# PEER: float32 one-hots and single products, sums copied out of PSUM, routing picks by four heads with one operand in PSUM

## The chip, the cores and the metric

The kernel runs on one core of one Trainium2 chip. The metric is the device time of one execution in microseconds (us), lower is better; several executions are taken, and the median is reported.

## The reference, cut to what matters

The program is a small network over 256 tokens of width 1024: an RG-LRU mixer, a PEER layer, a FoX attention mixer, a second PEER layer, and then a block with three branches and a dense FFN. Only the two PEER layers are touched. Each has 16384 experts (128 x 128), 8 heads, and picks 16 experts per head and token:

```python
q = (xc @ q_w).reshape(TOKEN_CHUNK, PEER_HEADS, 2, PEER_HALF)
s1 = jnp.einsum('thd,hnd->thn', q[:, :, 0], subkey1).astype(jnp.float32)
s2 = jnp.einsum('thd,hnd->thn', q[:, :, 1], subkey2).astype(jnp.float32)
v1, i1 = lax.top_k(s1, PEER_TOPK)
v2, i2 = lax.top_k(s2, PEER_TOPK)
cand = (v1[..., :, None] + v2[..., None, :]).reshape(...)
top_s, top_c = lax.top_k(cand, PEER_TOPK)
e1 = jnp.take_along_axis(i1, top_c // PEER_TOPK, axis=-1)
e2 = jnp.take_along_axis(i2, top_c % PEER_TOPK, axis=-1)
expert = e1 * PEER_KEYS + e2
g = jax.nn.softmax(top_s, axis=-1)
u = jnp.take(expert_u, expert, axis=0)
act = jax.nn.gelu(jnp.einsum('thkd,td->thk', u, xc).astype(jnp.float32), approximate=False)
w = (g * act).astype(xc.dtype)
return jnp.einsum('thk,thkd->td', w, jnp.take(expert_v, expert, axis=0))
```

## The kernel before, in words

**Dense evaluation.** The kernel gathers no expert. For every one of 128 rows e of the expert grid it computes the activations of that row's 128 experts for all 256 tokens, applies gelu and keeps them in the SBUF array W (128 partitions x 128 rows x 256 tokens). The routing turns into a matrix of gates of the same shape, which multiplies W, and W then multiplies expert_v. A product of two float32 matrices is made of three float32r matmuls on split operands (hi·hi, hi·lo, lo·hi: `mm3`, `proj`); one row e takes 8 x 3 = 24 matmuls of 128x256. The weights come as 512 KB units over the SP queue (`raw`), ACT rounds them to `whi`, and POOL (or DVE) subtracts to get `wlo` (`Stream`).

**A PEER layer** (`peer`) has four stretches. (1) 16 query tiles are projected; from tile 4 on, `q_scores` multiplies the one before with its subkeys: two matmuls per call with plain float32 operands, 128 moving columns each. (2) The loop `for e in range(P)` runs over rows 0 to 95 (`NL = NLOW = 96`): 24 matmuls, a gelu into `W[:, e]`, and between them routing and one-hot work. (3) Rows 96 to 127 go through two small buffers `act` in the space of x, are multiplied with gates that already lie in W, and for two groups of four tokens per row `low(g)` fetches the gates of rows 0 to 95 from DRAM (`gdram`, on the ACT queue) and multiplies them in on DVE or POOL. (4) W times expert_v accumulates over 128 units.

**Routing** (`routing`) runs for token halves t = 0, 1 on DVE. `sides` takes the best 16 of 128 scores for two lists of a head (max, max_index, match_replace). `heads(t)` then works on all eight heads: five additions of candidates, four `sums` (the best 16 of 54 candidates), and the picks: comparisons `ge`, multiplications into `w` and reductions over 8 x 16 x 16 = 2048 elements a partition, all operands in SBUF. `softmax` makes the gates, and after `WAIT` = 4 turns TensorE transposes the two expert indices and the gate; ACT and DVE copy them into `tp`, the gate as a rounded part and a remainder.

**One-hots** (`onehots`). `make(i)` builds for two tokens A (128x256: is this the first index) with one DVE instruction and `gg` (128x256 for each token: one-hot of the second index times the gate, as rounded part and remainder side by side) with one instruction per token; the iota they compare with lies in a PSUM bank. `use` multiplies: one float32r matmul of 128x256 per token, four tokens (a group) into a `ps2` tile of two banks. The rounded part and the remainder stand in separate columns, so ACT copies one out and DVE adds the other, once for rows 0 to 95 (`stage`, then to `gdram`) and once for rows 96 to 127 (W). A layer has 256 tokens, so 64 groups. At row e = NL - 2 = 94 whatever is left of `onehots` is issued at once.

**What sets the order.** The program text issues instructions in the order of these generators; a planner then fixes each engine's order ahead of time, within dependencies, and the engines run their lists in order. In the text, `route()` advances the routing while a rough clock in the program puts DVE behind TensorE; `due` spreads the groups over the rows that are left (`left / (NL - ENDS - e)` a row, cut to 1.0 behind the loop); at row `SCRATCH` = 58 the rest of the routing is forced, since its scratch space in W begins at that row. `tp` lies in columns 1024 to 2047 of x, `act` in 1536 to 2047: gelu of row 96 may write `act` only when the last one-hot that reads there is made.

Of the kernel before, what the change touches and what calls it, by code (L numbers as in the profile page):

```python
# [22 lines left out]
SCRATCH = 58  # L23
WAIT = 4
LAGS = 1
OHB = (2, 3)
# [290 lines left out]
class Kern:  # L317
# [582 lines left out]
    def peer(self, l, ps, gs, shift=None, tasks=None):  # L900
# [6 lines left out]
        with tc.tile_pool(name="W", bufs=1, side="right", reuse_waits="tile") as wp:  # L907
# [22 lines left out]
            step1, sa = half(c0 + 17, 0, 8), half(c0 + 17, 1, 8)  # L930
            scr = [[half(c0 + 18 + i, j) for j in range(2)] for i in range(2)]
            ge, w = [part(c0 + u, 2048).rearrange("p (h k j) -> p h k j", h=8, k=16) for u in (20, 28)]
            gf = half(c0 + 36, 0)
            sm = half(c0 + 36, 1, 2)[:, :, 0:8]
# [33 lines left out]
            def heads(t):  # L968

                v1, v2 = top[:, 0:16:2], top[:, 1:16:2]  # L970
# [7 lines left out]
                i1, i2 = idx[:, 0:16:2], idx[:, 1:16:2]  # L978
                nc.vector.tensor_copy(step1[:, :, 0:1], i1[:, :, 0:1])
                nc.vector.tensor_sub(step1[:, :, 1:16], i1[:, :, 1:16], i1[:, :, 0:15])  # L980
                yield
                for h in range(0, 8, 2):
                    yield from sums(h)
                nc.vector.tensor_copy(cf, cu)
                sh = [P, 8, 16, 16]

                def pick(out, table):
                    nc.vector.tensor_mul(w, ge, table)
# [4 lines left out]
                def slots(s):  # L993
                    return er[t][:, s].rearrange("p (h k) -> p h k", h=8)
# [4 lines left out]
                yield from pick(sa, self.first_step[:, None, None, :].to_broadcast(sh))  # L999
                yield from pick(slots(0), step1[:, :, None, :].to_broadcast(sh))  # L1000
                nc.vector.tensor_sub(bf, cf, sa)
                nc.vector.tensor_tensor(ge, bf[:, :, :, None].to_broadcast(sh),
                                        self.iota_f[:, None, None, 0:16].to_broadcast(sh), op=ALU.is_equal)
# [3 lines left out]
            def softmax(t):  # L1007
                g3 = gf.rearrange("p (h k) -> p h k", h=8)
                nc.vector.tensor_sub(g3, ts, ts[:, :, 0:1].to_broadcast([P, 8, 16]))
                nc.scalar.activation(g3, g3, AF.Exp)  # L1010
                nc.vector.tensor_reduce(sm[:, 0], g3, axis=AX.X, op=ALU.add)
                nc.vector.reciprocal(sm[:, 1], sm[:, 0])
                nc.vector.tensor_mul(g3, g3, sm[:, 1, :, None].to_broadcast([P, 8, 16]))
                for _ in range(WAIT):
                    yield "wait"
# [3 lines left out]
                o = slice(t * P, (t + 1) * P)  # L1019
# [930 lines left out]
```

## Time and profile before

| | us |
|---|---|
| runs of the kernel before: median (lowest, highest of 3) | 2624.33 (2618.27, 3353.15) |
| the profiled execution's own time | 2615.78 |
| span of its profile | 2613.9 |
| mean granted TensorE clock, of full speed | 0.971 |

The rows below come from this one profiled execution. The matmul durations in rows are latencies of pipelined instructions (about 0.28 us, while one starts every 0.12 us), so rates are read from counts in a window; PE's busy time is the union of them. [...] All instructions share line 225 (a helper that records them), so groups are told apart by tile names: `pb` and `ps` are PSUM tiles, `A` and `g` the one-hots, `x` the staging space, `W` the array W or the scratch in it.

### The profile page before, as it was taken

What the parts mean: (1) busy time and instruction counts of PE and PEld (TensorE: products, weight loads), DVE (VectorE), ACT (ScalarE), POOL (GpSimd) and SP (SyncE); (2) the same over time, 40 slices, a digit from 0 to 9 for tenths busy, and PEclk for the clock granted to TensorE, in tenths of its full rate; (3) what the DMA queues carried; (4) which work ended last, traced back from release to release, by engine and by line L of the source; (5) the groups of instructions that cost most, each with busy time, mean ns of one, the idle gap of its engine ahead of it and who ended that gap; (6) DMA issues with size and microseconds to landing.
All of it is one profiled execution on the core that took longest, in us unless ns stands there. A gap on an engine that the chain in (4) does not pass through costs nothing.

```text
span 2613.9 us, 48560 instructions
## 1 busy us (share of the span) xinstructions
PE 2443.3 (93%) x18984; PEld 2369.2 (91%) x18984; DVE 1887.6 (72%) x3552; ACT 1248.1 (48%) x2028; POOL 994.5 (38%) x600
## 2 busy tenths in 40 slices
PE   6879799997899999999997999899999999999998
PEld 5779799997899999888897999789999998999996
DVE  8797997778778765664779877876555557557774
ACT  3655355553434444554544555435444444444553
POOL 5377777762321200231476877340000015203310
PEclk9889999998999999999998999899999999999999
DMA  7755457677788875542454766686555554365564
GB/s 267 287 164 181 143 168 216 214 210 242 241 307 312 311 241 184 156 151 89 150 166 145 210 212 212 202 282 223 182 182 185 184 174 147 112 195 162 186 184 139
DMA packets 164133, 517.38 MB, mean 198 GB/s; under 512 B 18224, under 2 KB 51136, under 8 KB 162880
## 3 DMA queue, kind: packets, MB, share of 16 engines
q1 hardware_dynamic: 117072, 425.77, 51.5%
q10 hardware_dynamic: 38768, 59.14, 6.6%
q0 software_dynamic: 8064, 29.36, 3.5%
q8 instruction: 149, 2.44, 0.4%
q14 instruction: 80, 0.66, 0.1%
HBM read 484.85 MB, written 29.36 MB: 197 GB/s over the span
## 4 chain that ended last, share of the span: by engine, by line
PE 63%; DVE 17%; DMA 8%; issue 7%; POOL 3%; ACT 1%; ACTq 0%; POOLq 0%; DVEq 0%; SPq 0%
PE pb L225 32%; PE ps L225 31%; DVE W L225 7%; DMA x<-gdram 5%; DVE mraw L225 2%; DVE wlo L225 1%; POOL W L225 1%; DVE hl L225 1%; DVE g L225 1%; DMA raw<-pv 1%; DVE tt L225 1%; DVE x L225 1%; DVE mod_mix L225 1%; POOL wlo L225 1%; DVE A L225 1%
## 5 line engine op out<-in xcount | busy, mean ns | idle before, releaser
L225 ACT CAST whi<-raw 128x1024 fp32r<-128x1024 f32 x741 | 777.2, 1050 | 909.2 <-PE ps L225 309.2
L225 POOL TENSOR_TENSOR wlo<-raw,whi 128x1024 fp32r<-128x1024 f32 x284 | 714.0, 2521 | 433.6 <-ACT whi L225 371.7
L225 DVE TENSOR_TENSOR wlo<-raw,whi 128x1024 fp32r<-128x1024 f32 x473 | 610.3, 1291 | 368.7 <-ACT whi L225 366.0
L225 PE MATMUL pb<-hh,whi 128*128 128x256 f32 (+1 forms) x2832 | 810.2, 288 | 34.2 <-ACT x L225 13.0
L225 PE MATMUL pb<-hl,whi 128*128 128x256 f32 (+1 forms) x2832 | 808.8, 286 | 4.7 <-DVE hl L225 4.6
L225 PE MATMUL pb<-hh,wlo 128*128 128x256 f32 (+1 forms) x2832 | 802.1, 285 | 4.9 <-POOL wlo L225 2.5
L225 PE MATMUL ps<-hh,whi 128*128 128x256 f32 x2416 | 686.8, 285 | 11.7 <-ACT hh L225 6.1
L225 PE MATMUL ps<-hh,wlo 128*128 128x256 f32 x2416 | 686.0, 284 | 11.3 <-DVE wlo L225 7.9
L225 PE MATMUL ps<-hl,whi 128*128 128x256 f32 x2416 | 688.4, 285 | 4.7 <-DVE hl L225 4.7
L225 PEld LDWEIGHTS pb<-hh,whi 128*128 128x128 f32 x2832 | 544.7, 193 | 40.5 <-ACT x L225 17.4
L225 PEld LDWEIGHTS pb<-hl,whi 128*128 128x128 f32 x2832 | 545.5, 193 | 5.8 <-DVE hl L225 5.8
L225 PEld LDWEIGHTS pb<-hh,wlo 128*128 128x128 f32 x2832 | 544.7, 193 | 6.3 <-POOL wlo L225 3.3
L225 PEld LDWEIGHTS ps<-hh,wlo 128*128 128x128 f32 x2416 | 461.1, 191 | 15.6 <-DVE wlo L225 10.6
L225 PEld LDWEIGHTS ps<-hh,whi 128*128 128x128 f32 x2416 | 460.6, 191 | 12.8 <-ACT hh L225 6.6
L225 PEld LDWEIGHTS ps<-hl,whi 128*128 128x128 f32 x2416 | 459.1, 190 | 7.1 <-DVE hl L225 5.7
L225 DVE SCALAR_TENSOR_TENSOR g<-pb,x 128x256 fp32r<-128x256 f32 x512 | 222.6, 476 | 0.0
L225 POOL TENSOR_TENSOR W<-W 128x256 f32<-128x256 f32 x12 | 9.3, 774 | 517.7 <-ACT W L225 517.7
L225 PE MATMUL ps<-g,A 128*128 128x256 f32 x512 | 140.1, 299 | 28.1 <-DVE W L225 24.1
L225 DVE TENSOR_TENSOR A<-pb,x 128x256 fp32r<-128x256 f32 x256 | 107.8, 421 | 54.0 <-PE ps L225 52.9
L225 POOL TENSOR_TENSOR W<-W,x 128x384 f32<-128x384 f32 (+1 forms) x66 | 80.2, 1227 | 125.5 <-DMA x<-gdram 94.9
L225 PEld LDWEIGHTS ps<-g,A 128*128 128x128 f32 x512 | 96.4, 199 | 33.0 <-issue 26.2
L225 DVE TENSOR_TENSOR W<-W,x 128x256 f32<-128x256 f32 (+1 forms) x126 | 88.4, 720 | 35.1 <-DMA x<-gdram 20.5
(398 smaller groups left out, 3009.1 us busy)
## 6 DMA issues: line engine op xcount, KB each, us to landing
raw<-pu SPq DMA_DIRECT2D x256, 512.0 KB, 3.9
raw<-pv SPq DMA_DIRECT2D x256, 512.0 KB, 4.1
gdram<-x ACTq DMA_DIRECT2D x128, 192.0 KB, 3.3
x<-gdram ACTq DMA_DIRECT2D x128, 192.0 KB, 3.8
raw<-w_rest SPq DMA_DIRECT2D x40, 512.0 KB, 3.7
raw<-pq SPq DMA_DIRECT2D x32, 512.0 KB, 4.2
mraw<-mod_mix SPq DMA_DIRECT2D x24, 512.0 KB, 5.5
raw<-fox_qkv SPq DMA_DIRECT2D x24, 512.0 KB, 3.7
```

Of the source, the lines that this page charges most:

```text
L225: return f(*args, **kw)
```

## The change

PEER's one-hots become plain float32: `gg` has only the gate itself (128x128 per token), the product of a token is one float32 matmul of 128 moving columns, a group fills one bank, and ACT copies both parts of it out; DVE's additions go. The gate is no longer split, so one ACT copy fills `tp` (three parts in place of four). `heads(t, q)` works on four heads at a time, as soon as their `sides` are there; each of its two-operand instructions has one operand in PSUM (`v2p`, `i1p`, `sap`, `firstp`, `ge`, `mxp`, and the iota). The scratch shrinks (24.5 rows in place of 36.5) and moves from row 58 to 62, `WAIT` is 12 for t = 0 and stays 4 for t = 1, there are four buffers of A and of g (before: 2 and 3), and `due` is cut to 1.5.

```diff
-SCRATCH = 58
-WAIT = 4
+SCRATCH = 62
+WAIT = (12, 4)
-OHB = (2, 3)
+OHB = (4, 4)
...
-            ge, w = [part(c0 + u, 2048).rearrange("p (h k j) -> p h k j", h=8, k=16) for u in (20, 28)]
+            w = part(c0 + 20, 1024).rearrange("p (h k j) -> p h k j", h=4, k=16)
-            tp = xf[:, 1024:2048].rearrange("p (s t) -> p s t", s=4)
+            tp = xf[:, 1024:1792].rearrange("p (s t) -> p s t", s=3)
...
             def sides(h, t):
-                nc.vector.tensor_copy(idx[:, 2 * h:2 * h + 2], iu[:, 2 * h:2 * h + 2])
...
-            def heads(t):
+            def heads(t, q):
+                hs, hd = slice(4 * q, 4 * q + 4), slice(8 * q, 8 * q + 8)
+                sh = [P, 4, 16, 16]
+                v1, v2 = top[:, hd][:, 0::2], top[:, hd][:, 1::2]
+                nc.vector.tensor_copy(v2p, v2)
...
-                        cand[:, :, o:o + n * nb].rearrange("p h (a b) -> p h a b", b=nb),
-                        v1[:, :, a0:a1, None].to_broadcast([P, 8, n, nb]),
-                        v2[:, :, None, 0:nb].to_broadcast([P, 8, n, nb]), op=ALU.add)
+                        cand[:, hs, o:o + n * nb].rearrange("p h (a b) -> p h a b", b=nb),
+                        v1[:, :, a0:a1, None].to_broadcast([P, 4, n, nb]),
+                        v2p[:, :, None, 0:nb].to_broadcast([P, 4, n, nb]), op=ALU.add)
...
+                nc.vector.tensor_copy(idx[:, hd], iu[:, hd])
+                nc.vector.tensor_copy(i1p, i1)
...
-                nc.vector.tensor_tensor(ge, cf[:, :, :, None].to_broadcast(sh),
-                                        self.first[:, None, None, :].to_broadcast(sh), op=ALU.is_ge)
+                nc.vector.tensor_tensor(ge, cf[:, hs, :, None].to_broadcast(sh),
+                                        firstp[:, None, None, :].to_broadcast(sh), op=ALU.is_ge)
...
             def softmax(t):
-                for _ in range(WAIT):
+                for _ in range(WAIT[t]):
                     yield "wait"
...
-                nc.scalar.copy(tp[:, 0:2, o], ps[:, 0:2 * P].rearrange("p (s t) -> p s t", s=2))
-                hi = oh.tile([P, 2, P], F32R, name="A", bufs=OHB[0])[:, 0]
-                nc.scalar.copy(hi, ps[:, 2 * P:3 * P])
-                nc.scalar.copy(tp[:, 2, o], hi.bitcast(F32))
-                nc.vector.tensor_sub(tp[:, 3, o], ps[:, 2 * P:3 * P], hi.bitcast(F32))
+                nc.scalar.copy(tp[:, :, t * P:(t + 1) * P], ps[:, 0:3 * P].rearrange("p (s t) -> p s t", s=3))
...
             def routing():
-                    yield from heads(t)
+                        if h % 4 == 3:
+                            yield from heads(t, h // 4)
...
                 def make(i):
-                    A = oh.tile(b2, F32R, name="A", bufs=OHB[0])
-                    gg = oh.tile([P, 2, 2, P], F32R, name="g", bufs=OHB[1])
+                    A = oh.tile(b2, F32, name="A", bufs=OHB[0])
+                    gg = oh.tile(b2, F32, name="g", bufs=OHB[1])
...
-                        nc.vector.scalar_tensor_tensor(gg[:, k], both, tp[:, 1, n:n + 1],
-                                                       tp[:, 2:4, n, None].to_broadcast(b2),
+                        nc.vector.scalar_tensor_tensor(gg[:, k], io, tp[:, 1, n:n + 1],
+                                                       tp[:, 2, n, None].to_broadcast([P, P]),
...
                 def use():
-                    if i % 2 == 0:
-                        bank[0] = self.ps2()
+                    g = i // 2
+                    bank = picked[:, g % 2 * 512:g % 2 * 512 + 512]
-                        nc.tensor.matmul(bank[0][:, o * T:(o + 1) * T], A[:, k], gg[:, k].rearrange("p s e -> p (s e)"),
-                                         start=True, stop=True)
+                        nc.tensor.matmul(bank[:, o * P:(o + 1) * P], A[:, k], gg[:, k], start=True, stop=True)
...
-                        for o, e in ((st, slice(0, NL)), (W[:, NL:, 4 * g:4 * g + 4], slice(NL, P))):
-                            nc.scalar.copy(o, pv[:, 0, e])
-                            nc.vector.tensor_add(o, o, pv[:, 1, e])
+                        nc.scalar.copy(st, pv[:, 0:NL])
+                        nc.scalar.copy(W[:, NL:, 4 * g:4 * g + 4], pv[:, NL:])
...
+                consts = self.bank(spare)
+                io, firstp, mxp = consts[:, 0:P], consts[:, 128:144], consts[:, 144:152]
+                v2p, i1p, sap = [consts[:, o:o + 64].rearrange("p (h k) -> p h k", h=4) for o in (192, 256, 320)]
+                picked = self.ps2()
+                ge = self.ps2().rearrange("p (h k j) -> p h k j", h=4, k=16)
...
-                        due = min(due, 1.0)
+                        due = min(due, 1.5)
```

## Rows read from the trace of the kernel before

**Rows 1.** The page, part 1: busy us (share of the span) xinstructions, per engine.

```profile
PE 2443.3 (93%) x18984; PEld 2369.2 (91%) x18984; DVE 1887.6 (72%) x3552; ACT 1248.1 (48%) x2028; POOL 994.5 (38%) x600
```

**Rows 2.** Busy time by stretch, PE PEld DVE ACT POOL, PEclk, DMA; first PEER layer.

```profile
core 0: us, PE busy (x) PEld busy (x) DVE busy (x) ACT busy (x) POOL busy (x), PEclk, DMA share, GB/s
220.00:260.00 40.00, 40.00 (x341) 40.00 (x340) 23.56 (x110) 21.63 (x50) 30.24 (x13) 1.00 0.61 198
...
256.30:583.50 327.20, 310.97 (x2551) 310.03 (x2550) 278.02 (x779) 171.96 (x320) 242.84 (x96) 0.97 0.63 189
583.50:612.00 28.50, 15.25 (x79) 13.01 (x78) 25.05 (x61) 8.93 (x20) 0.74 (x1) 0.65 0.58 172
612.00:704.40 92.40, 85.30 (x687) 82.69 (x687) 72.33 (x82) 36.71 (x56) 39.73 (x33) 1.00 0.84 270
...
390.00:575.00 185.00, 185.00 (x1551) 184.98 (x1550) 142.88 (x372) 105.90 (x210) 137.48 (x58) 1.00 0.71 214
```

**Rows 3.** The same view, second PEER layer.

```profile
1332.20:1659.00 326.80, 310.48 (x2552) 309.53 (x2551) 277.68 (x780) 171.95 (x320) 243.09 (x96) 0.97 0.62 190
1659.00:1687.00 28.00, 15.70 (x81) 13.46 (x80) 25.29 (x62) 8.93 (x20) 0.26 (x1) 0.65 0.63 181
1687.00:1778.40 91.40, 85.33 (x685) 83.67 (x684) 71.55 (x81) 38.92 (x60) 40.26 (x33) 0.98 0.83 267
```

**Rows 4.** PE in order of time, 285:328: start, duration, instruction, idle before and releaser.

```profile
287.06 0.39 PE L225 MATMUL pb<-hh,whi 128*128 128x256 f32 x1 [2.09 <-ACT W L225]
308.57 0.44 PE L225 MATMUL pb<-ident,W 128*128 128x128 f32 x1 [8.31 <-DVE W L225]
...
326.71 0.58 PE L225 MATMUL pb<-hh,whi 128*128 128x256 f32 x1 [4.59 <-DVE x L225]
```

**Rows 5.** PE in order of time, 590:613.

```profile
592.84 1.19 PE L225 MATMUL ps<-g,A 128*128 128x256 f32 x4 [3.81 <-DVE W L225]
598.19 1.19 PE L225 MATMUL ps<-g,A 128*128 128x256 f32 x4 [4.16 <-DVE W L225]
600.85 2.00 PE L225 MATMUL ps<-g,A 128*128 128x256 f32 x4 [1.46 <-ACT x L225]
605.71 1.20 PE L225 MATMUL ps<-g,A 128*128 128x256 f32 x4 [2.86 <-DVE W L225]
```

**Rows 6.** Waits, 625:720: engine and tile, releaser, us in total, times, longest.

```profile
POOL W L225 <- DMA x<-gdram: 41.6, 19, 3.9
PEld pb L225 <- ACT x L225: 9.7, 13, 1.8
```

**Rows 7.** PE in order of time, 222:246: plain float32 matmuls of q_scores.

```profile
222.75 0.60 PE L225 MATMUL pb<-W 128*128 128x128 f32 x4
...
245.90 0.60 PE L225 MATMUL pb<-W 128*128 128x128 f32 x4
```

**Rows 8.** DVE groups by shape, 390:575: busy us, mean ns, idle before and releaser.

```profile
L225 DVE SCALAR_TENSOR_TENSOR g<-pb,x 128x256 fp32r<-128x256 f32 x185 | 80.4, 476 | 0.0
L225 DVE TENSOR_TENSOR A<-pb,x 128x256 fp32r<-128x256 f32 x93 | 39.3, 423 | 24.7 <-PE ps L225 24.3
L225 DVE TENSOR_TENSOR x<-x,ps 128x384 f32<-128x384 f32 x46 | 25.2, 548 | 0.2 <-ACT x L225 0.2
L225 DVE TENSOR_TENSOR W<-W,ps 128x128 f32<-128x128 f32 x47 | 13.4, 286 | 18.5 <-ACT W L225 18.5
```

**Rows 9.** DVE in order of time, 284:352: two-operand instructions, both operands in SBUF.

```profile
285.84 4.04 DVE L225 TENSOR_TENSOR W<-W,first 128x2048 f32<-128x2048 f32 x1
...
294.47 2.21 DVE L225 TENSOR_TENSOR W<-W 128x128 f32<-128x128 f32 x1
...
342.86 0.32 DVE L225 TENSOR_TENSOR W<-W 128x128 f32<-128x128 f32 x1
...
346.37 2.28 DVE L225 TENSOR_TENSOR W<-W,first 128x2048 f32<-128x2048 f32 x1
```

**Rows 10.** DVE's waits, 220:260.

```profile
DVE W L225 <- ACT W L225: 15.1, 10, 3.0
```

More of the change, by code (lines that the diff above doesn't have):

```diff
@@ L929, in peer @@
             cf, bf = half(c0 + 16, 0, 8), half(c0 + 16, 1, 8)
-            step1, sa = half(c0 + 17, 0, 8), half(c0 + 17, 1, 8)
+            step1 = half(c0 + 17, 0, 8)
             scr = [[half(c0 + 18 + i, j) for j in range(2)] for i in range(2)]
-            ge, w = [part(c0 + u, 2048).rearrange("p (h k j) -> p h k j", h=8, k=16) for u in (20, 28)]
-            gf = half(c0 + 36, 0)
-            sm = half(c0 + 36, 1, 2)[:, :, 0:8]
+            w = part(c0 + 20, 1024).rearrange("p (h k j) -> p h k j", h=4, k=16)
+            gf = half(c0 + 24, 0)
+            sm = half(c0 + 24, 1, 8)[:, :, 0]
             act = xf[:, 1536:2048].rearrange("p (s t) -> p s t", s=2)
-            tp = xf[:, 1024:2048].rearrange("p (s t) -> p s t", s=4)
+            tp = xf[:, 1024:1792].rearrange("p (s t) -> p s t", s=3)
             def stage(g, n):
@@ L966, in sums @@
                 yield from tops([ts[:, i] for i in r], [cu[:, i] for i in r], [cand[:, i] for i in r], CAND, scr[0])
-            def heads(t):
-                v1, v2 = top[:, 0:16:2], top[:, 1:16:2]
+            def heads(t, q):
[3 more added lines that the diff above has]
+                nc.vector.tensor_copy(v2p, v2)
                 for a0, a1, nb, o in RANKS:
@@ L973, in heads @@
                     nc.vector.tensor_tensor(
-                        cand[:, :, o:o + n * nb].rearrange("p h (a b) -> p h a b", b=nb),
-                        v1[:, :, a0:a1, None].to_broadcast([P, 8, n, nb]),
-                        v2[:, :, None, 0:nb].to_broadcast([P, 8, n, nb]), op=ALU.add)
+                        cand[:, hs, o:o + n * nb].rearrange("p h (a b) -> p h a b", b=nb),
+                        v1[:, :, a0:a1, None].to_broadcast([P, 4, n, nb]),
+                        v2p[:, :, None, 0:nb].to_broadcast([P, 4, n, nb]), op=ALU.add)
                     yield
-                i1, i2 = idx[:, 0:16:2], idx[:, 1:16:2]
-                nc.vector.tensor_copy(step1[:, :, 0:1], i1[:, :, 0:1])
-                nc.vector.tensor_sub(step1[:, :, 1:16], i1[:, :, 1:16], i1[:, :, 0:15])
+                nc.vector.tensor_copy(idx[:, hd], iu[:, hd])
+                i1, i2 = idx[:, hd][:, 0::2], idx[:, hd][:, 1::2]
+                d1 = step1[:, hs]
+                nc.vector.tensor_copy(i1p, i1)
+                nc.vector.tensor_copy(d1[:, :, 0:1], i1[:, :, 0:1])
+                nc.vector.tensor_sub(d1[:, :, 1:16], i1[:, :, 1:16], i1p[:, :, 0:15])
                 yield
-                for h in range(0, 8, 2):
+                for h in range(4 * q, 4 * q + 4, 2):
                     yield from sums(h)
-                nc.vector.tensor_copy(cf, cu)
-                sh = [P, 8, 16, 16]
+                nc.vector.tensor_copy(cf[:, hs], cu[:, hs])
                 def pick(out, table):
-                    nc.vector.tensor_mul(w, ge, table)
+                    nc.vector.tensor_tensor(w, ge, table, op=ALU.mult)
                     yield
@@ L993, in slots @@
                 def slots(s):
-                    return er[t][:, s].rearrange("p (h k) -> p h k", h=8)
-                nc.vector.tensor_tensor(ge, cf[:, :, :, None].to_broadcast(sh),
-                                        self.first[:, None, None, :].to_broadcast(sh), op=ALU.is_ge)
+                    return er[t][:, s].rearrange("p (h k) -> p h k", h=8)[:, hs]
+                nc.vector.tensor_tensor(ge, cf[:, hs, :, None].to_broadcast(sh),
+                                        firstp[:, None, None, :].to_broadcast(sh), op=ALU.is_ge)
                 yield
[L999 to L1003, printed above, removed]
+                yield from pick(sap, self.first_step[:, None, None, :].to_broadcast(sh))
+                yield from pick(slots(0), d1[:, :, None, :].to_broadcast(sh))
+                nc.vector.tensor_sub(bf[:, hs], cf[:, hs], sap)
+                nc.vector.tensor_tensor(ge, bf[:, hs, :, None].to_broadcast(sh),
+                                        io[:, None, None, 0:16].to_broadcast(sh), op=ALU.is_equal)
                 yield
@@ L1108, in peer @@
                 spare = self.ring.pop(0)
-                io = self.bank(spare)[:, 0:P]
+                consts = self.bank(spare)
+                io, firstp, mxp = consts[:, 0:P], consts[:, 128:144], consts[:, 144:152]
+                v2p, i1p, sap = [consts[:, o:o + 64].rearrange("p (h k) -> p h k", h=4) for o in (192, 256, 320)]
                 nc.vector.tensor_copy(io, self.iota_f)
+                nc.vector.tensor_copy(firstp, self.first)
+                picked = self.ps2()
+                ge = self.ps2().rearrange("p (h k j) -> p h k j", h=4, k=16)
                 nc.sync.dma_start(sk, a[f"sk_{l}"].rearrange("p (h n) -> p h n", h=16))
```

19 lines of the change are left out of this document (9 added, 10 removed).

## The prediction

> **What bounds the kernel now.** Part 1 of the page comes first: TensorE is busy 93% of the span, DVE 72%, ACT and POOL less than half [rows 1]. That average does not say what one PEER layer is bound by, so I cut the layer into stretches [rows 2] and looked at how many matmuls start in each. From 390 to 575 us TensorE is busy all of the time at full clock and starts 1551 matmuls in 185.00 us, one every 0.1193 us; DVE is busy 142.88 us of it. This is the steady state of the row loop with one-hot products in it, and TensorE is its bound. The reader should take that rate as a ruler: a stretch's length less its matmuls times 0.1193 us is TensorE time lost. For the first layer that gives
>
> - rows 0 to 95, 256.3 to 583.5: 327.2 - 2551 x 0.1193 = 22.9 us lost;
> - the tail, 583.5 to 612: 28.5 - 79 x 0.1193 = 19.1 us lost;
> - the rows from 96 on, 612 to 704.4: 92.4 - 687 x 0.1193 = 10.4 us lost.
>
> The second layer repeats it with 22.3, 18.3 and 9.7 us [rows 3]. Next I asked what TensorE waited for. In the first stretch the two largest gaps are 8.31 us before a transpose of the routing results, which DVE had not finished, and 4.59 us before a projection whose PSUM bank was held until DVE had copied the gate's remainder into `tp` (DVE x) [rows 4]; the rest is 2.09 us for a gelu, small gaps, and matmuls at half clock after them (mean clock 0.97 [rows 2]). In the tail there are hardly any projections left to run: TensorE multiplies four products and waits again for DVE, 3.81, 4.16, 2.86 us [rows 5], while DVE is busy 25.05 of 28.50 us and the mean clock falls to 0.65 [rows 2]. These are groups that the text had issued by row 94 and that came after it in TensorE's list. In the last stretch the waits are for gates on their way back from DRAM (41.6 us on POOL) and for ACT's gelu [rows 6].
>
> **Part 1, the product: a cost.** A token's product was one float32r matmul of 256 columns, 0.1193 us in the steady state. It becomes one plain float32 matmul of 128 columns. The kernel before has the same thing in `q_scores`: two such matmuls, profiled as four records, once per query tile. From 222.75 to 245.90 us seven tiles pass, 3.307 us each [rows 7]; 24 projections take 24 x 0.1193 = 2.863, which leaves 0.444 us for two, 0.222 us for one. The additional cost is 0.103 x 256 = 26.3 us a layer, **52.6 us in all**. It lies wholly on the path, as TensorE is the bound there. The ends: 0 if a plain product costs what the old one does, and 0.325 us x 256 = 83 us a layer if the products meet the half clock (0.444 us). I take the row of `q_scores`, which stands in the same kind of stream, at full clock.
>
> **Part 2, DVE's share of a group: hidden.** 185 products are 46.25 groups, so DVE spent 142.88 / 46.25 = 3.09 us on a group, and a group came every 4.00 us. The two additions (0.548 + 0.286) go; an instruction for `g` (0.476) shrinks to 128 elements, between 0.286 (another 128x128 instruction that reads PSUM) and 0.476 [rows 8]. Two of A and four of g then make 2 x 0.423 + 4 x 0.286 = 2.0 us, at the worst 2.75. I take 2.0, as that row has the same size and operand. ACT's two copies stay as they are. Nothing of this is a gain in the steady state, where DVE already waits 24.3 us for TensorE [rows 8]; it decides whether the tail remains.
>
> **Part 3, the tail: a gain.** TensorE gets slower per group (0.48 to 0.89 us) and DVE faster (3.1 to 2.0), so DVE is no longer what the groups run behind. 64 groups over some 70 rows is 0.9 a row, 2.86 + 0.8 = 3.7 us of TensorE against 1.8 of DVE. The larger cut of `due` (1.5) lets a delayed group be caught up. I let 2 us of the tail stay (the last copies before `act` comes free): gain 17.1 + 16.3 = **33.4 us**. The ends are 0 and 37.4.
>
> **Part 4, routing: a gain.** The transposes of t = 0 move 8 turns further back in TensorE's list, 8 x 2.86 = 23 us of projections, where the wait was 8.31 us. Queued behind the transposes on TensorE are the projections, and for their results wait ACT's `tp` copy and the first one-hots: those start later, which the rates of part 3 allow. The bank of the transposes is now freed by ACT alone, so the 4.59 us go. DVE also comes earlier: while the queries are projected it waits 15.1 us for scores [rows 10], and the first four heads' additions and picks can stand there. The picks were five two-operand instructions of 2048 elements per half of the tokens with both operands in SBUF, 2.28 us at best and 4.04 otherwise; a 128x128 one took 0.32 and once 2.21 [rows 9]. The new ones have one operand in PSUM and half the elements; between 0 and 5 x 1.76 = 8.8 us per half may be won. Against that stand some 34 more small instructions a layer, at most 0.32 us each, 11 us. Both lie on DVE beside TensorE's projections and I count them as nothing; if that cover were gone, they would come in at +11 to -18 us a layer. Of the 22.9 and 22.3 us I let 4 stay, for the gelu gap of 2.09 and a first wait for one-hots: gain **37.2 us**, with ends 0 and 45.2.
>
> **Part 5, nothing.** Rows 96 to 127 keep their 10.4 and 9.7 us: the same 64 fetches on the ACT queue, the same POOL and DVE products. The tail let a few of them run ahead; I bound that by 5 us a layer in either direction. The other scratch rows, the buffer counts and the smaller `tp` move no work that is late.
>
> **The sum.** 52.6 - 33.4 - 37.2 = -18.0 us against the profiled execution: 2615.8 - 18.0 = **2598 us**. The profiled execution lies just below the lowest of the three runs shown (2618.27) and 8.5 us below their median, 2624.33; I forecast for an execution like it.
>
> **The rivals.**
> - *The tail stays* (slower). Each engine's order is fixed ahead, and nothing in the rows shows that DVE's load made the tail: DVE waited for TensorE in the steady state [rows 8], so it may be the order alone. Then 2615.8 + 52.6 - 37.2 = 2631 us. For it: TensorE had work all the time before the tail. Against it: DVE was busy 88% of the tail. It decides once more than 18.0 / 33.4 = 54% of the tail remains.
> - *Routing stalls as well*: the transposes meet DVE just as late, eight rows on. With the tail that is 2615.8 + 52.6 = 2668 us. Against it: the wait of 8.31 us is shorter than 23 us.
> - *The product is no dearer than before*: 2598 - 52.6 = 2545 us. Only rows 7 speak, and they speak against it.
> - *All stalls go*, with 5 us a layer in the rows from 96 on: 2598 - 4 - 8 - 10 = 2576 us. For it: DVE loses much of its load.
> - [...]
>
> **How the numbers follow.** The forecast gets 0.68, with a range of its own of 2582 to 2614 (what stays of the stalls, and the product at 0.20 to 0.25 us). The tail that stays gets 0.15, both stalls 0.05, a product at the old price 0.04, all stalls gone 0.06, four passes 0.02. The range for 8 in 10 is 2572 to 2640: it takes in the case with the tail and the one without any stall, and leaves out the rest. A change of 2%, 52 us, is about what a measurement of this kernel can tell from none: below 2563 lies only the cheap product (0.04), above 2668 four passes and half of the case with both stalls (0.05), 0.91 between them. In words: a few us gained where TensorE waited, most of it paid back in dearer products.
>
> **What would show it.** The new product: between two of them in the stream some 0.22 us, and two records each. DVE's busy time in the row loop falls by about a third, the additions are gone from its groups. The clock in the row loop stays at 1.00, with no gap of 8.31 or 4.59 us before a transpose or the projection behind it. After row 95 the projections of rows 96 and on run on, with no stretch in which TensorE waits for DVE between products. From the end of the last query tile to the first product with expert_v it is 448.1 us today; I expect about 438. I am wrong if that stretch still holds a block of products after row 95, or if the products cost under 0.2 or over 0.25 us.

## The result, and the profile after

The changed kernel takes 2586.04 us (median of 4 runs, 2585.15 to 2592.58); the kernel before, run beside it, 2622.52 (4 runs, lowest 2618.27). The ratio is 0.9872, 95% interval [0.9847, 0.9896]; it leaves out one run of the kernel before that took 3353.15 us, 28% longer than the others. Between the two profiled executions it is 2585.15 against 2615.78 us, 30.6 us less, where 18 had been forecast.

The page of the kernel after, part 1, answers to [rows 1]:

```profile
PE 2473.5 (96%) x19496; PEld 2406.7 (93%) x19496; DVE 1688.1 (65%) x3364; ACT 1242.3 (48%) x2018; POOL 966.5 (37%) x596
```

TensorE is busy 30 us longer and the span is 31 us shorter: what it stood idle has gone down by some 60 us. The busy time by stretch of the kernel after, both PEER layers, shows where. The columns are those of [rows 2], PEclk the granted clock as a share of full speed; the first line is rows 0 to 95, the second rows 96 to 127, the third lies inside the first, and the last two are the second layer:

```profile
core 0: us, PE busy (x) PEld busy (x) DVE busy (x) ACT busy (x) POOL busy (x), PEclk, DMA share, GB/s
260.30:592.00 331.70, 331.70 (x2817) 331.54 (x2816) 183.63 (x674) 173.60 (x329) 227.60 (x96) 1.00 0.63 194
592.00:691.00 99.00, 92.71 (x753) 90.30 (x752) 81.77 (x93) 41.02 (x63) 40.97 (x32) 1.00 0.88 283
390.00:575.00 185.00, 185.00 (x1577) 185.00 (x1576) 82.58 (x271) 98.15 (x193) 121.45 (x52) 1.00 0.61 192
1316.30:1648.00 331.70, 331.70 (x2817) 331.54 (x2816) 184.38 (x676) 173.81 (x330) 227.78 (x96) 1.00 0.62 192
1648.00:1747.10 99.10, 92.13 (x750) 89.94 (x750) 81.07 (x92) 40.61 (x62) 43.68 (x32) 1.00 0.87 281
```

From the last query tile to the first product with expert_v it is 430.7 us (260.3 to 691.0), where it was 448.1; in the second layer 430.8, where it was 446.2. That is 17.4 + 15.4 = 32.8 us; the rest of the program takes 2.2 us more.

Rows 0 to 95 are now a stretch in which TensorE never stands still. 96 x 24 projections at 0.1193 us are 274.9 us, 256 products at 0.222 us are 56.8, together 331.7, the length of the stretch: nothing is lost, where 22.9 us and, in the tail, 19.1 us were lost. In rows 96 to 127, 99.0 - 32 x 24 x 0.1193 = 7.4 us are lost, where it was 10.4.

TensorE in order of time, kernel after:

```profile
309.01 0.49 PE L225 MATMUL pb<-ident,W 128*128 128x128 f32 x3
313.97 0.61 PE L225 MATMUL ps<-g,A 128*128 128x128 f32 x4
...
581.75 1.05 PE L225 MATMUL ps<-g,A 128*128 128x128 f32 x8
```

The transposes of t = 0 start at 309.01, hardly later than the 308.57 of [rows 4], but with nothing idle before them; the last products start at 581.75, before row 95, so there is no block of products after the row loop as in [rows 5].

DVE's groups by shape, 390 to 575, kernel after, to be read beside [rows 8]:

```profile
L225 DVE SCALAR_TENSOR_TENSOR g<-pb,x 128x128 f32<-128x128 f32 x176 | 52.9, 342 | 0.0
L225 DVE TENSOR_TENSOR A<-pb,x 128x256 f32<-128x256 f32 x88 | 37.0, 421 | 100.4 <-PE ps L225 100.4
```

The additions are gone, and DVE spends 82.58 us of 185 there, where it was 142.88. The last stretch still has the waits of [rows 6] (600 to 691, kernel after):

```profile
POOL W L225 <- DMA x<-gdram: 46.0, 22, 4.1
```

### The profile page after: what moved, and what is told of

The parts are those of the page before. It is cut to its first block, busy times and chain, and to the rows that moved or that the text cites. A ratio compares the mean times of both kernels' runs of the same rounds, so it can differ in the third digit from the quotient of the medians.

```text
span 2583.3 us, 49235 instructions
## 1 busy us (share of the span) xinstructions
PE 2473.5 (96%) x19496; PEld 2406.7 (93%) x19496; DVE 1688.1 (65%) x3364; ACT 1242.3 (48%) x2018; POOL 966.5 (37%) x596
## 4 chain that ended last, share of the span: by engine, by line
PE 71%; DVE 9%; DMA 7%; issue 7%; POOL 3%; ACT 1%; ACTq 0%; POOLq 0%; DVEq 0%
PE pb L225 37%; PE ps L225 34%; DMA x<-gdram 4%; DVE mraw L225 2%; DVE wlo L225 2%; DMA raw<-pv 1%; POOL W L225 1%; DVE W L225 1%; DVE hl L225 1%; DMA mraw<-mod_ffn 1%; POOL wlo L225 1%; ACT whi L225 1%; DVE mod_mix L225 1%; DVE tt L225 1%; DMA raw<-pu 0%
## 5 line engine op out<-in xcount | busy, mean ns | idle before, releaser
L225 POOL TENSOR_TENSOR wlo<-raw,whi 128x1024 fp32r<-128x1024 f32 x282 | 681.5, 2418 | 481.0 <-ACT whi L225 429.6
L225 DVE TENSOR_TENSOR A<-pb,x 128x256 f32<-128x256 f32 x256 | 107.0, 418 | 255.7 <-PE ps L225 223.8
L225 DVE SCALAR_TENSOR_TENSOR g<-pb,x 128x128 f32<-128x128 f32 x512 | 153.6, 341 | 0.0
L225 PE MATMUL ps<-g,A 128*128 128x128 f32 x1024 | 138.3, 274 | 0.0
L225 PEld LDWEIGHTS ps<-g,A 128*128 128x128 f32 x1024 | 127.0, 191 | 0.0
L225 POOL TENSOR_TENSOR W<-W,x 128x384 f32<-128x384 f32 x64 | 85.5, 1345 | 101.3 <-DMA x<-gdram 98.3
L225 ACT COPY x<-ps 128x384 f32<-128x384 f32 x128 | 61.4, 479 | 103.5 <-PE ps L225 103.3
```

Source lines behind the costliest of these rows:

```text
L225: return f(*args, **kw)
```

## The experiments

Three questions were open. Is it the product at 0.222 us that pays most of the gain back? Did the tail go because DVE has less to do? Which part of the routing's change took its stalls away? All times below are medians, with their ratio to the kernel before on the same chip; between runs on different chips the ratios are the fairer comparison. "..." marks where lines of an edit or of a view are left out.

### Each half of the change alone

The kernel before with the new one-hots, products and copies (`make`, `use` and the copy into `tp` are those of the kernel after); its routing stays, by eight heads and in SBUF. The edit to the kernel before, beside these:

```diff
-OHB = (2, 3)
+OHB = (4, 4)
...
-            tp = xf[:, 1024:2048].rearrange("p (s t) -> p s t", s=4)
+            tp = xf[:, 1024:1792].rearrange("p (s t) -> p s t", s=3)
```

> The kernel before with the new one-hots, products and sums alone; routing, its place in the order and the cut of due stay as before. Theory (DVE's share of a group made the tail, the order of the routing made the stalls): the tail of 19 us a layer is gone, the routing stalls of 22 us a layer stay, the dearer products cost 26 us a layer: 2615.8 + 52.6 - 37 = 2631 us, with the gap of 8.3 us before the first transpose still in the trace and no block of products after row 95. Rival (the order alone made the tail, DVE's share did not): nothing is won and the products are paid, 2668 us, with a tail of some 30 matmuls or more after row 95.

2623.8 us, ratio 1.0016 [0.9999, 1.0032]. TensorE in order of time:

```profile
308.77 0.45 PE L225 MATMUL pb<-ident,W 128*128 128x128 f32 x1 [8.30 <-DVE W L225]
...
361.04 1.50 PE L225 MATMUL ps<-g,A 128*128 128x128 f32 x8 [2.18 <-DVE g L225]
...
598.07 1.05 PE L225 MATMUL ps<-g,A 128*128 128x128 f32 x8
```

The routing's stall of 8.3 us stands as before. The last products come at 598.07 with no idle time before them: the tail has gone with this half alone. What it saves pays for the dearer products, and no more.

The routing alone; `ge`, whose tile of two banks the old products use here, lies in SBUF, and each pick's table in PSUM in its place. The edit to the kernel after, beside the old `make`, `use` and copies into `tp`:

```diff
-OHB = (4, 4)
+OHB = (2, 3)
...
+                stepp = consts[:, 152:168]
+                d1p, i2p = [consts[:, o:o + 64].rearrange("p (h k) -> p h k", h=4) for o in (384, 448)]
...
-                yield from pick(slots(0), d1[:, :, None, :].to_broadcast(sh))
+                yield from pick(slots(0), d1p[:, :, None, :].to_broadcast(sh))
```

> The changed kernel with the old one-hots, products (float32r, 256 columns, gate in two parts) and additions on DVE; routing by four heads, waits of 12 and 4, scratch at row 62 and cut of 1.5 as changed. The comparisons ge lie in SBUF here, since the products need the PSUM, and the tables they are multiplied with lie in PSUM instead. Theory: the stalls of the routing go (45 us), the tail stays, since DVE still spends 3.1 us on a group: 2615.8 - 45 = 2571 us. Rival (the order alone made the tail): tail and stalls go and the products cost what they did before, 2586 - 52.6 = 2533 us, which would be faster than both kernels.

2619.2 us, ratio 0.9986 [0.9972, 1.0]: no gain either. TensorE in order of time:

```profile
463.00 0.39 PE L225 MATMUL pb<-hh,whi 128*128 128x256 f32 x1 [1.35 <-ACT W L225]
468.66 0.33 PE L225 MATMUL pb<-ident,W 128*128 128x128 f32 x1 [2.52 <-DVE W L225]
472.30 0.47 PE L225 MATMUL pb<-ident,W 128*128 128x128 f32 x1 [3.31 <-DVE W L225]
474.74 0.58 PE L225 MATMUL pb<-hh,whi 128*128 128x256 f32 x1 [1.96 <-ACT W L225]
...
589.96 1.19 PE L225 MATMUL ps<-g,A 128*128 128x256 f32 x4 [4.72 <-DVE W L225]
...
597.53 1.19 PE L225 MATMUL ps<-g,A 128*128 128x256 f32 x4 [2.87 <-DVE W L225]
```

The stall before the first transposes is gone and the tail stays, as the edit has it. But the gain in the first rows comes back in the transposes of t = 1, which row 62 forces: TensorE waits 1.35 + 2.52 + 3.31 + 1.96 = 9.1 us there for a DVE that has the second half's routing and the old one-hots to do. So the halves change the time by +0.16% and -0.14%, and together by -1.28%. As I read the rows, the light one-hots make the room in DVE that the second routing needs: with them TensorE has no such wait in the kernel after.

### Which part of the routing's change

`WAIT` back to 4 for both halves of the tokens, in the kernel after:

```diff
-WAIT = (12, 4)
+WAIT = (4, 4)
```

> The changed kernel with a wait of 4 turns for both token halves. Theory (the place of the transposes in TensorE's list made the largest stall, together with DVE's lateness): a gap of up to 8 us comes back before the first transposes, with half-clock matmuls behind it, 2586 + 2 x 10 = 2606 us at most. Rival (DVE is early enough by the picks in fours, whatever the wait): no gap, 2586 us within 3.

2589.59 us, ratio 0.988 [0.9855, 0.9906], inside the interval of the change itself. One gap comes back:

```profile
291.14 0.33 PE L225 MATMUL pb<-ident,W 128*128 128x128 f32 x1 [3.05 <-DVE W L225]
```

The transposes are issued 18 us earlier than in the kernel after and wait 3.05 us: DVE is done with the routing at about 291, not at 308. The longer `WAIT` takes that wait away; 3.6 us in the medians is within what the runs can tell from none.

The kernel after with all operands of the picks in SBUF, still by four heads:

```diff
-            w = part(c0 + 20, 1024).rearrange("p (h k j) -> p h k j", h=4, k=16)
+            ge, w = [part(c0 + u, 1024).rearrange("p (h k j) -> p h k j", h=4, k=16) for u in (20, 24)]
...
-                io, firstp, mxp = consts[:, 0:P], consts[:, 128:144], consts[:, 144:152]
-                v2p, i1p, sap = [consts[:, o:o + 64].rearrange("p (h k) -> p h k", h=4) for o in (192, 256, 320)]
+                io = consts[:, 0:P]
+                firstp, mxp = self.first, half(c0 + 29, 1)[:, 0:8]
+                v2p, i1p, sap = [half(c0 + u, i)[:, 0:64].rearrange("p (h k) -> p h k", h=4) for u, i in ((17, 1), (28, 1), (29, 0))]
...
-                ge = self.ps2().rearrange("p (h k j) -> p h k j", h=4, k=16)
```

> The changed kernel with every operand of the picks in SBUF (the picks still by four heads, ge and its neighbours in scratch); only the one-hots still read their iota from PSUM. Theory (the operand in PSUM saves time on DVE alone, beside TensorE's projections): DVE's two-operand instructions of 1024 elements go from about 1.2 us to between 1.2 and 3 us, POOL's subtractions stretch in the same place, and the time stays at 2586 us within 5. Rival (contention of DVE and POOL makes the weights late): TensorE waits for wlo or for the transposes while the picks run, 2595 us or more.

2650.12 us, ratio 1.0109 [1.0083, 1.0134]: 64 us more than the kernel after, and slower than the kernel before. TensorE, ACT, DVE and POOL in order of time, of this kernel:

```profile
290.04 0.58 PE L225 MATMUL pb<-hh,whi 128*128 128x256 f32 x1 [8.71 <-ACT W L225]
...
323.04 0.69 PE L225 MATMUL pb<-ident,W 128*128 128x128 f32 x2 [5.50 <-DVE W L225]
...
343.80 0.80 PE L225 MATMUL ps<-g,A 128*128 128x128 f32 x2 [13.63 <-DVE g L225]
```

```profile
287.04 0.31 ACT L225 ACTIVATE W<-W 128x128 f32<-128x128 f32 x1 [11.69 <-DVE W L225]
```

```profile
288.73 3.07 DVE L225 TENSOR_TENSOR W<-W,first 128x1024 f32<-128x1024 f32 x1
...
327.20 1.21 DVE L225 TENSOR_TENSOR W<-W,first 128x1024 f32<-128x1024 f32 x1
```

```profile
290.99 28.30 POOL L225 TENSOR_TENSOR wlo<-raw,whi 128x1024 fp32r<-128x1024 f32 x10 [0.28 <-ACT whi L225]
...
344.51 2.37 POOL L225 TENSOR_TENSOR wlo<-raw,whi 128x1024 fp32r<-128x1024 f32 x1 [22.83 <-ACT whi L225]
```

And the same picks in the kernel after, with `ge` in PSUM:

```profile
284.00 1.20 DVE L225 TENSOR_TENSOR W<-ps,first_step 128x1024 f32<-128x1024 f32 x1
...
291.73 1.20 DVE L225 TENSOR_TENSOR W<-ps,W 128x1024 f32<-128x1024 f32 x1
```

One instruction, two durations: it took 3.07 us while POOL made `wlo`, 1.21 us at 327, when POOL stood still (its next instruction, at 344.51, has waited 22.83 us). With an operand in PSUM it took 1.20 us with POOL at work. This is where two SBUF operands cost the time: on DVE, and from there on TensorE, which waits 8.71 + 5.50 + 13.63 = 27.8 us in this layer. The first of these comes by way of ACT: the exponential of `softmax` had stood 11.69 us in ACT's list for DVE's input, and the gelu and the rounding of weights stood behind it.

Eight heads at a time as in the kernel before, but one operand of each pick in PSUM, on top of the first experiment:

```diff
-                yield from pick(slots(1), i2[:, :, None, :].to_broadcast(sh))
+                yield from pick(slots(1), i2p[:, :, None, :].to_broadcast(sh))
...
+                more = self.ps2()
+                v2p, i1p, step1, i2p, sap = [more[:, o:o + P].rearrange("p (h k) -> p h k", h=8) for o in range(0, 640, P)]
```

> The kernel of the first experiment (new products, routing by eight heads, waits of 4, scratch at row 58), where now each two-operand instruction of the picks has one operand in PSUM (tables in PSUM, ge in SBUF). Theory (the operand in PSUM makes the routing early, the cut in fours does little by itself): the gap of 8.3 us before the transposes shrinks below 4 us, the time falls from 2624 to 2600 us or less. Rival (it is the cut in fours, which uses DVE's idle time while the queries are projected): 2612 us or more.

2597.55 us, ratio 0.9928 [0.9903, 0.9952], 26 us under the first experiment (23 by the ratios):

```profile
307.62 0.45 PE L225 MATMUL pb<-ident,W 128*128 128x128 f32 x1 [3.48 <-DVE W L225]
...
321.82 0.33 PE L225 MATMUL pb<-ident,W 128*128 128x128 f32 x1 [1.12 <-DVE W L225]
```

Of the 38 us between the first experiment and the kernel after, the operand in PSUM is some 25; fours, `ge` in PSUM and the constants share the rest, and they were not taken apart further, but for the constants:

```diff
-WAIT = (12, 4)
+WAIT = (4, 4)
...
-OHB = (4, 4)
+OHB = (2, 3)
...
-                        due = min(due, 1.5)
+                        due = min(due, 1.0)
```

> The changed kernel with the order constants of before: waits of 4 and 4, buffers of A and g 2 and 3, due cut to 1.0. Theory (operands and sizes made the gain, the constants do not): 2590 us within 5, as with the wait of 4 alone. Rival (fewer buffers and the smaller cut let the groups fall behind): a block of products after row 95, 2600 us or more.

2588.91 us, ratio 0.9895 [0.9864, 0.9926]. Buffer counts, the cut of `due` and `WAIT` together make no difference that these runs can measure.

### The price of the product

The kernel after with A and g as float32r. The gates' lower bits are left out (they are rounded, with no remainder); each product stays 128 columns wide:

```diff
-                    A = oh.tile(b2, F32, name="A", bufs=OHB[0])
-                    gg = oh.tile(b2, F32, name="g", bufs=OHB[1])
+                    A = oh.tile(b2, F32R, name="A", bufs=OHB[0])
+                    gg = oh.tile(b2, F32R, name="g", bufs=OHB[1])
```

> The changed kernel with A and g as float32r: one float32r matmul of 128 columns a token. It leaves out the lower bits of the gate, which is rounded. Theory (the float32 product stands on the path at its full price, since TensorE is busy without a gap in the row loop): a token's product falls from 0.22 to some 0.11 us, 512 of them, and the time with it: 2586 - 56 = 2530 us. Rival (with cheaper products DVE's one-hots or POOL's subtractions become the bound): less than half of that, 2560 us or more.

2527.17 us, ratio 0.9649 [0.9628, 0.967], 59 us under the kernel after. Busy time by stretch, and the group of the products in it:

```profile
390.00:575.00 185.00, 185.00 (x1565) 184.92 (x1564) 91.55 (x268) 104.40 (x204) 132.41 (x58) 1.00 0.70 222
```

```profile
L225 PE MATMUL ps<-g,A 128*128 128x128 f32 x172 | 24.9, 260 | 0.0
```

The ruler gives both prices. Here 172 products stand among 1565 matmuls; the other 1393 are projections but for 3 transposes, so a product takes (185 - 1390 x 0.1193) / 172 = 0.11 us. In the kernel after, 1577 records hold 352 of products, two each: (185 - 1225 x 0.1193) / 176 = 0.221 us. So a plain float32 product costs twice what a float32r one of the same width costs, and the 512 products cost 512 x 0.11 = 56 us more than rounded ones, close to the 59 measured. It all lies on the path. This is the fastest kernel here, but with gates of fewer bits; no kernel with whole gates was measurably faster than the changed one.

### Why the tail went

DVE's additions back into the kernel after. ACT's copies stay, and DVE adds zeros from PSUM to what they leave, two instructions a group as before:

```diff
-                        nc.scalar.copy(st, pv[:, 0:NL])
-                        nc.scalar.copy(W[:, NL:, 4 * g:4 * g + 4], pv[:, NL:])
+                        for o, e in ((st, slice(0, NL)), (W[:, NL:, 4 * g:4 * g + 4], slice(NL, P))):
+                            nc.scalar.copy(o, pv[:, e])
+                            nc.vector.tensor_add(o, o, zp[:, 0:e.stop - e.start].rearrange("p (e o) -> p e o", o=1).to_broadcast([P, e.stop - e.start, 4]))
...
+                zp = consts[:, 384:480]
+                nc.vector.memset(zp, 0.0)
```

> The changed kernel with two more DVE instructions for each group: after each of the two copies out of PSUM, a zero from PSUM is added, in the size and place of the old additions. Theory (DVE's share of a group made the tail): DVE goes from about 1.8 to 2.6 us of the 3.6 to 4 us that a group has, so it still keeps up, no block of products stands after row 95 and the time stays at 2586 us within 8. Rival (the additions themselves, between copy and store, hold a group up, whatever DVE's load): the tail is back, 2610 us or more.

2676.03 us, ratio 1.0214 [1.0191, 1.0238], 90 us more than the kernel after; the theory had it unchanged. Busy time by stretch, DVE's group of the first addition (390 to 575), and TensorE after the row loop:

```profile
390.00:575.00 185.00, 179.73 (x1477) 178.48 (x1476) 98.36 (x323) 90.23 (x173) 119.21 (x50) 0.97 0.60 180
600.00:640.00 40.00, 30.72 (x144) 25.14 (x143) 34.70 (x101) 9.53 (x26) 1.36 (x2) 0.66 0.55 167
```

```profile
L225 DVE TENSOR_TENSOR x<-x,pb 128x384 f32<-128x384 f32 x34 | 18.8, 552 | 81.4 <-ACT x L225 81.2
```

```profile
618.95 2.43 PE L225 MATMUL ps<-g,A 128*128 128x128 f32 x8 [0.74 <-ACT W L225]
...
634.78 2.43 PE L225 MATMUL ps<-g,A 128*128 128x128 f32 x8 [0.74 <-ACT W L225]
```

There is a tail again, and a longer one (12 of the 64 groups come after row 95, seven in the kernel before), though DVE is busy only 98.36 of 185 us. It is not short of time: it stands 81.2 us at the addition, which waits for ACT's copy, which waits for TensorE's products; and behind the addition in DVE's list stand the one-hots of the next products. A quarter of the groups is lost to that round (34 additions of `stage`, so 34 groups, in 185 us; in the kernel after 176 products, 44 groups), and what is left over comes behind the loop.

To tell the wait from the work, the same additions are issued one group later, when the copies have long been made (`flush` holds the two additions and the store to `gdram` of the group that has waited longest). The edit to the kernel with the additions back:

```diff
-                        for o, e in ((st, slice(0, NL)), (W[:, NL:, 4 * g:4 * g + 4], slice(NL, P))):
+                        if ready:
+                            flush()
+                        for o, e in parts:
                             nc.scalar.copy(o, pv[:, e])
-                            nc.vector.tensor_add(o, o, zp[:, 0:e.stop - e.start].rearrange("p (e o) -> p e o", o=1).to_broadcast([P, e.stop - e.start, 4]))
-                        nc.scalar.dma_start(self.gdram[:, g], st.rearrange("p e t -> p (e t)"))
+                        ready.append((g, pv, st, parts))
...
```

> The run with the additions put back (2676 us), with each group's two additions and its store issued one group later, so that DVE meets them when ACT's copies are long done. The same work. Theory now (the wait for the hand-over made the tail): DVE's wait of 81 us in 185 us for ACT's copies is nearly gone and the time falls to 2600 us or less. Rival (the additions cost by their number, or by the planner's order alone): 2650 us or more.

2584.51 us, ratio 0.9868 [0.9838, 0.9898]: as fast as the kernel after, with two more instructions in each of 128 groups.

```profile
390.00:575.00 185.00, 185.00 (x1577) 185.00 (x1576) 125.10 (x401) 97.66 (x193) 122.14 (x52) 1.00 0.63 193
```

```profile
L225 DVE TENSOR_TENSOR x<-x,pb 128x384 f32<-128x384 f32 x44 | 24.3, 553 | 1.8 <-ACT x L225 1.1
```

DVE now works 125.10 us of the same stretch, 27 more than in the run with the tail, and there is no tail. In this form the wait makes it, not the load. The edit moves the store with the additions, and the store waits for them in ACT's list; which of the two lists that stood still costs more was not taken apart.

The load by itself, the other way round: the kernel after with `g` built 256 wide (only the first half is used), no additions, buffers as before:

```diff
-OHB = (4, 4)
+OHB = (2, 3)
...
-                    gg = oh.tile(b2, F32, name="g", bufs=OHB[1])
+                    gg = oh.tile([P, 2, 2, P], F32, name="g", bufs=OHB[1])
...
```

> The changed kernel with each g built 256 wide, as before, the second half unused, and no additions (buffers 2 and 3, which cost nothing in the run with the old constants). DVE's busy time per group rises by about as much as the two additions took, but no DVE instruction waits for ACT. Theory now (not DVE's load but the additions made the tail: DVE's list stands still at them until TensorE and ACT have handed the group over): no block of products after row 95, 2586 us within 8. Rival (the forecast's own step, DVE's load per group): products after row 95 and 2610 us or more, as with the additions put back.

2599.67 us, ratio 0.9932 [0.9905, 0.9959], 13.6 us above the kernel after, more than expected. The stretch has no idle time, and a remnant of a tail stands after row 95, which ends at 589 us (four groups):

```profile
390.00:575.00 185.00, 185.00 (x1574) 185.00 (x1572) 110.96 (x301) 97.05 (x190) 124.19 (x53) 1.00 0.62 191
```

```profile
602.05 1.16 PE L225 MATMUL ps<-g,A 128*128 128x128 f32 x8 [1.12 <-ACT W L225]
```

From the last query tile to the first product with expert_v the layers take 433.6 and 434.8 us, 3 and 4 us more than in the kernel after; the other half of the 13.6 us lies outside them and is not explained. Nor is the remnant put down to load alone: with the additions one group later DVE is busier (125.10 us against 110.96) and no product comes after row 95, but the buffers there are four and four.

Last, the same delay by one group in the old form: the routing alone, above, with its additions (old products, whole gates) one group later. The edit to that kernel:

```diff
-                        for o, e in ((st, slice(0, NL)), (W[:, NL:, 4 * g:4 * g + 4], slice(NL, P))):
+                        if ready:
+                            flush()
+                        for o, e in parts:
                             nc.scalar.copy(o, pv[:, 0, e])
-                            nc.vector.tensor_add(o, o, pv[:, 1, e])
-                        nc.scalar.dma_start(self.gdram[:, g], st.rearrange("p e t -> p (e t)"))
+                        ready.append((g, pv, st, parts))
...
```

> The second experiment (new routing, old products at 0.12 us, gate in two parts, additions on DVE) with the additions issued one group later. It computes all that the kernel before does. Theory now: the tail of the second experiment (products up to 607 us, after row 95) goes, and with it most of 19 us a layer: 2619 - 35 = 2584 us, or down to 2540 us if the 10 us of routing stalls a layer at 463 to 481 us go as well and DVE keeps up. Rival (DVE at 3.1 us a group is too slow beside a group every 3.6 us, whatever the waits): the tail stays, 2610 us or more.

2601.22 us, ratio 0.9939 [0.9918, 0.9959]: 18 us under the routing alone, 12 by the ratios, and between the two theories. From the last query tile to the first product with expert_v it is 439.2 + 437.2 us in the two layers, where it was 445.8 + 442.2.

```profile
390.00:575.00 185.00, 178.06 (x1467) 177.18 (x1466) 146.09 (x381) 97.98 (x191) 131.25 (x56) 0.98 0.65 198
```

```profile
468.47 0.33 PE L225 MATMUL pb<-ident,W 128*128 128x128 f32 x1 [2.97 <-DVE W L225]
...
594.37 2.00 PE L225 MATMUL ps<-g,A 128*128 128x256 f32 x4 [3.86 <-DVE g L225]
...
597.73 2.00 PE L225 MATMUL ps<-g,A 128*128 128x256 f32 x4 [1.36 <-DVE g L225]
```

The tail stays, as the rival had it. Busy time in its block of products, first in the routing alone (seven groups), then here (six):

```profile
584.60:608.60 24.00, 9.57 (x30) 6.67 (x28) 22.09 (x58) 5.83 (x16) 1.55 (x1) 0.61 0.51 153
```

```profile
581.20:602.90 21.70, 10.00 (x26) 6.24 (x24) 19.31 (x50) 5.17 (x15) 2.10 (x1) 0.60 0.49 147
```

TensorE in the tail now waits mostly for `g` itself, where in [rows 5] it was for an addition's tile, but a group takes no less: 3.6 us, where it was 3.4. DVE is busy 89% of the block (92% in the routing alone). So in this old form (products of 256 columns, gates in two parts) DVE's load holds the tail even without the wait; in the block it includes the first products with gates for the rows that follow. The products at 0.119 us would make this form 52 us cheaper on TensorE than the kernel after; the old one-hots on DVE take that back, and some 15 us more.

## Why the prediction was right

The forecast was 2598 us, the result 2586; 18 us less were forecast, 30.6 came between the profiled executions. By its own steps:

**Part 1, the product.** Right: 0.222 us forecast, 0.221 measured, and wholly on the path, as the rounded product shows by giving 59 us back. This is the largest term of the sum, and `q_scores` in the old kernel [rows 7] was the row to take it from. No run shows the four passes that have 0.02 among the chances: a product has two records and takes 0.221 us.

**Part 2, DVE's share of a group.** 2.0 us forecast; 82.58 us for 44 groups are 1.9. An instruction for `g` takes 0.342 us and not the 0.286 of the row that was used; the durations overlap (176 of 0.342 are 60.2 us, and the group is busy 52.9), so that the sum comes out all the same.

**Part 3, the tail.** The amount was right (33.4 us forecast; all of 37.4 went, 19.1 + 18.3). The step that gave it, "DVE is no longer what the groups run behind", argued from DVE's share of a group, is half of the cause. For it: with the old products DVE is busy 92% of the block of products after the loop, and with the additions one group later the block stays, at 3.6 us a group. Against it: with the new products the load does not decide. With the additions back DVE was busy 98.36 us of the stretch for 34 groups, where it had been 142.88 for 46 before the change, and the tail was longer; with the same additions one group later DVE was busy 125.10 us and there was none. What the step left out is the addition's place in DVE's list: it stood waiting for a round from DVE over TensorE and ACT, with the next one-hots behind it. A row for this was there: DVE's wait of 18.5 us for ACT before the smaller addition in [rows 8]. (The 24.3 us beside it are a wait for a buffer of A that a product frees; that is slack, as the prediction read it.) The rival that the tail stays, because "it may be the order alone", has this much for it: the same work in two orders gives a tail of 12 groups and none. The change takes both away, the additions and half the width of `g`; how much of the old tail each of them made is not shown. Why the round takes 5.4 us a group with the additions put back (185 / 34) is open.

**Part 4, routing.** 37.2 us forecast, all of 22.9 + 22.3 = 45.2 went; again the cause was another one. "The transposes of t = 0 move 8 turns further back" is worth 3.6 us in the medians (2589.59 with `WAIT` at 4), no more than the runs can tell from none. The step that failed is "both lie on DVE beside TensorE's projections and I count them as nothing": the picks with both operands in SBUF are the larger part of the stalls; in the kernel before one took 4.04 us at 285.84 [rows 9], while POOL ran, and one of the same size 2.28 at 311.07, while POOL stood still. With one operand in PSUM on top of the first experiment some 25 us go; with two in SBUF in the kernel after 64 us come. The bound for the case without cover, "+11 to -18 us a layer", was too small: it counted DVE's own instructions, five of 1.76 us a half. The 32 us a layer that it did cost are, in the first layer, mostly three waits of TensorE (27.8 us), and the longest, 13.63 us, is for a `g` that stands in DVE's list behind the delayed routing. The two stalls named in [rows 4] did go; neither is in the trace of the kernel after. Nor is the half clock behind them: the kernel before was granted 0.50 from 309 to 311 us and from 326.5 to 329, the kernel after 1.00 from 300 to 330.

**Part 5, rows from 96 on.** They lose 7.4 us where 10.4 were forecast, within the 5 us a layer it was bounded by. The waits for gates from DRAM stand, 46.0 us on POOL (22 times; before 41.6).

**The sum.** 4 + 2 + 10.4 = 16.4 us of stalls were forecast to remain in the first layer, and 7.4 did; in the second 15.7 were, and 99.1 - 91.6 = 7.5 did. That is 17 us more gained; 2.2 us are lost outside the two stretches. 18.0 + 17.2 - 2.2 = 33.0, against 30.6 measured; of the difference, some 1.3 us a layer are matmul records missing from the trace of the kernel before (3317 counted of at least 128 x 24 + 256 = 3328), which the ruler took for losses. The rival "all stalls go", 2576 us, was a little nearer than the forecast (9 us off the profiled execution, the forecast 13): it was right for rows 0 to 95, and took 5 us a layer for the last rows, where it is 7.4. That the forecast comes so near is partly luck: the price of the product was worked out and right, but the gains of parts 3 and 4 came in nearly the size forecast with the causes only half named.

## What to carry to other kernels

An engine that runs its list in order stands still behind an instruction that waits for a round over other engines, as DVE did here for 81.2 of 185 us (1.1 with the additions a group later): where a profile shows it idle part of the time and yet late at the end, look for that instruction and issue it one round later. Look at the engine's busy share in the late block as well: where it is near full there, as with the old products here (89%), the delay alone leaves the block standing, and work has to go. While POOL works on SBUF, give each two-operand DVE instruction one operand in PSUM (1.20 us here, where two in SBUF took 3.07), and price an instruction with two in SBUF by what waits behind it and not by its own stretch. Two halves of a change that each bring nothing can bring all of it together: test them together too.

## What was not expected of the hardware

A DVE instruction of 128x1024 with two SBUF operands took 1.21 us when POOL stood still and 3.07 us when POOL ran; small ones lost far more in proportion. DVE's groups of 128x32 by shape, 210 to 345, first in the kernel after with its picks in SBUF, then in the kernel after itself:

```profile
L225 DVE TENSOR_TENSOR W<-W 128x32 f32<-128x32 f32 x8 | 8.0, 1004 | 0.0
```

```profile
L225 DVE TENSOR_TENSOR W<-W,pb 128x32 f32<-128x32 f32 x6 | 1.1, 177 | 0.0
```

1004 ns against 177 in the mean. POOL paid as well. Its group of `wlo`, 260 to 320, in the same two kernels, 2774 ns against 2402:

```profile
L225 POOL TENSOR_TENSOR wlo<-raw,whi 128x1024 fp32r<-128x1024 f32 x18 | 49.4, 2774 | 13.0 <-ACT whi L225 12.9
```

```profile
L225 POOL TENSOR_TENSOR wlo<-raw,whi 128x1024 fp32r<-128x1024 f32 x21 | 50.4, 2402 | 12.8 <-ACT whi L225 12.0 <-DMA raw<-pu 0.4 <-PE pb L225 0.2
```

The operand in PSUM cost nothing visible: 1.20 us, where the same size in SBUF took 1.21 undisturbed.
